# A hybrid decoder step on one core: the Pool mixer's map as a plain float32 product, with a new order of the pieces up to attention

## The chip, the cores and the metric

The kernel runs on one core of a Trainium2 chip. The metric is device microseconds of one execution, as the median of several runs. Times of single instructions come from one profiled execution of the same program, whose own time is given beside them.

## The reference

One layer with a prompt of 1024 tokens and eight sample tokens of one step each, which share the weights. Cut to what matters:

```python
h = rmsnorm(x, g_mix)
u = h @ w_in                              # 1024 -> 512 (a) + 512 (val) + 512 (gate)
a_ext = concat([pool_hist, a])            # group A: trailing windows of 2, 4, 8, 16 tokens
d = [win_sum_g / cnt_g - a_g for g in range(4)]        # 128 channels each
ya = (einsum('blgc,gcd->blgd', d, w_map) + b_map) * scale
yb = silu(layernorm(causal_conv31(val * sigmoid(gate))))    # group B
x = x + concat([ya, yb]) @ w_out
k, v = rmsnorm(mem) @ w_k, rmsnorm(mem) @ w_v          # 256 memory tokens, 4 heads
x = x + softmax(rmsnorm(x) @ w_q @ k.T / 16) @ v @ w_o
x = x + (silu(h2 @ w_gate) * (h2 @ w_up)) @ w_down     # h2 = rmsnorm(x)
y = rmsnorm(x, g_final)
```

The sample tokens go through the same products; their attention uses a cache of its own. All is float32. The outputs are y, the new states of the windows and of the convolution, and k and v.

## The kernel before

**Layout.** Channels lie on the 128 partitions, tokens along the free axis: T = 1032 columns, the 512 even and the 512 odd tokens of the prompt and the 8 samples. A product over all tokens is made in three pieces of 344 columns.

**Three passes.** Operands of products are split into a high and a low half in the reduced type fp32r, and a product is the sum of three passes (high x high, high x low, low x high). `step3` (L457) emits them: nine matmuls of 344 columns for one 128x128 block of a weight. The high half of a tensor is a copy on ACT or POOL (L346, L348), the low half a subtraction on DVE or POOL (L357, L359). For some weight blocks the low half is made by DMA instead (`split_by_dma`, L362 on): the negated high half is written first (a second copy on ACT, L368, or POOL, L370), then a DMA issued by POOL (L375) adds the weight from HBM to it. NOT_BY_DMA and BY_DMA name the blocks.

**The planner.** Each step is given to `Program.add` with the engines that can do it, a cost on each, what it reads and what it writes. `Program.order` then lists all steps by a simulated time: it takes the step that can start first, the earlier created one among near equals, and gives each an engine and a buffer. Every engine runs its instructions in the order so found, and the number of buffers of a kind (2 for product sums of the kind mm, 3 for raw weights, 2 for split weights, 19 large operands, 3 scratch) decides too when a step can start. So a cost moves no work by itself; it moves choices. ORDER is a string of pieces, in which they are created: A mixer inputs, g and v the gates and values of the convolution, C and D the convolution's taps (its sums `cacc` on DVE, L663), W windows, M the window's map, K and V keys and values of the memory, O and B the two halves of the output projection (`oa` and `ob`), L LayerNorm, q, S, T, P attention of the prompt, a to e that of the samples, Y and Z states. Behind ORDER stand the projection w_o, the gate stage and the down stage.

**Weights.** `w_take` hands over the next split block and keeps up to LEAD blocks more in preparation (`w_prep` splits, `w_load` fetches the raw block).

**The Pool mixer.** `windows` (L777) adds shifted copies of the input `a` for a window of 2, 4, 8 or 16 (L790 to L795, on POOL or DVE) and makes the mean minus the token itself (L802 to L804, always DVE): tile `win`. It is then split in two halves, tile `dop`. `mixer_out` (L841) multiplies `dop` by its block of the map (tile `pmap`, nine matmuls) and evicts with bias and scale on ACT (`yf`, L848); `yf` is split into `opa`, an operand of `oa` with the four blocks of w_out_a. The map's weight is one of the sequence of split blocks, between other weights.

**Beside it.** Keys (`kps`, L827) use a block of w_k for 24 matmuls of 256 columns; a piece K has two blocks. Values (`vps`, L901) use a block of w_v for 24 matmuls of 512 columns in two groups of 12; a piece V has four blocks. The LayerNorm of the convolution needs the sum of all its channels (`ysum`, L682), two products with a matrix of ones in plain float32 (`mean_ps`, L868, `rstd_ps`, L487) and gives the operands `opb` of `ob`.

Of the kernel before, what the change touches and what calls it, by code (L numbers as in the profile page):

```python
# [88 lines left out]
class Program:  # L89
# [4 lines left out]
    SIGNAL, SIGNAL_PE, SAME = 0.2, 0.29, {"DVE": 0.12, "ACT": 0.1}  # L94

    def __init__(self, capacity):
        self.capacity = capacity
        self.tasks, self.writer, self.readers, self.later = [], {}, {}, 0

    def add(self, engines, emit, r=(), w=(), lock=False, func=None, nbytes=0):  # L100
        t = Task()
        t.engines = engines
# [140 lines left out]
def hybrid_step_kernel(ctx: ExitStack, tc: tile.TileContext, io):  # L243
# [119 lines left out]
    def split_by_dma(dst, key, src, n, r, again, again_keys, pool_too=False):  # L363
# [11 lines left out]
        add({"Pool": 1.04}, lambda e: e.dma_start(dst(1), again(), accum_op=ALU.add), [key(1)] + again_keys, [key(1)], nbytes=4 * P * n)  # L375
# [31 lines left out]
    def w_load():  # L407
        i = state["loaded"]
        if i >= state["upto"]:
            return  # L410
        name, j = seq[i]
        width = 512 if name == "pool_map" else 1024
        raw = buf(f"raw{i}", "raw", (P, 1024))
        dma(lambda: raw[:, :width], lambda: io[name][j][:, :width], 512 * width, w=[(raw,)])
        raws[i] = (raw, width)
        state["loaded"] += 1

    def w_prep():
        i = state["prepped"]
        raw, width = raws.pop(i)  # L420
        name, j = seq[i]
        w = buf(f"w{i}", "op" if name in WIDE or i >= len(seq) - 4 else "w", (P, 2, 1024), F32R)
        if name in BY_DMA and i not in NOT_BY_DMA:
            split_by_dma(lambda p: w[:, p, :width], lambda p: (w, p), lambda: raw[:, :width], width, [(raw,)],
                         lambda: io[name][j][:, :width], [], name not in ("w_dn", "w_dn2"))
        else:
            split(lambda p: w[:, p, :width], lambda p: (w, p), lambda: raw[:, :width], width, [(raw,)])
        preps[i] = w
        state["prepped"] += 1
# [21 lines left out]
    def step3(ps, w, wkeys, cols, x, k, first, last, spans=range(NCH), keys=None):  # L451
# [8 lines left out]
        add({"PE": 0.146 * 3 * len(spans)}, emit, list(wkeys) + (keys or [(x, 0), (x, 1)]),  # L460
# [313 lines left out]
    a2 = [op_buf(f"a{i}") for i in range(2)]  # L774
    dops = {}

    def windows(g):  # L777
# [3 lines left out]
        tmp = op_buf(f"win{g}")  # L781
        add({"DVE": 0.07}, lambda e: e.tensor_copy(st_pool()[:, g, :, 15], ab[:, ai, SEQ:T]), [ak, (side, "pool")], [(side, "pool", g)])
# [24 lines left out]
        dops[g] = op_r(f"dop{g}")  # L807
        split(lambda p: dops[g][:, p], lambda p: (dops[g], p), cur, T, [ck])
# [11 lines left out]
    def keys(q):  # L820
        ps = mm_buf(f"kps{q}", 1)
        for i in range(2):
            w, wkeys = w_take("w_k")
            for k in range(KT):
# [4 lines left out]
                add({"PE": 0.327}, emit, wkeys + [(memg[k // 4], p, k % 4) for p in range(2)], [(ps,)])  # L829
# [62 lines left out]
    def values(c):  # L892
        ps = mm_buf(f"vps{c}", 2)
        for kk in range(4):
            w, wkeys = w_take("w_v")
            for k in (2 * kk, 2 * kk + 1):
# [6 lines left out]
                add({"PE": 1.3}, emit, wkeys + [(memg[k // 4], p, k % 4) for p in range(2)], [(ps,)])  # L903
# [76 lines left out]
    def scores(n):  # L980
# [23 lines left out]
        add({"PE": 1.31}, emit, [(qop[2 * h + dt], p) for dt in range(2) for p in range(2)] + [(kk, p, o) for p in range(2)], [pk])  # L1004
# [42 lines left out]
    def pv(n):  # L1047
# [4 lines left out]
        for c in range(2):  # L1052
# [8 lines left out]
            add({"PE": 1.3}, emit, [(v, 0), (v, 1)] + [(pT[h][m], p, c) for p in range(2) for m in range(2)], [(ps, c)])  # L1061
# [209 lines left out]
    def product(w, cols, xs, steps=1):  # L1271
# [254 lines left out]
    rsqrt_rows("Rf", Rf, RF, xss2, [(xss2,)], ones_d, 0, T)  # L1526
    for f in range(AHEAD):
        first_two(f)
    for f in range(FF_TILES):
# [5 lines left out]
        else:  # L1535
            fixed["DVE"] = 0.148
# [28 lines left out]

    last_w = {block: w_take(block[0]) for block in last_blocks}
# [3 lines left out]
    def last_down(c, n):  # L1570
# [19 lines left out]
        for w, keys, ks in ((wa, ka, range(4)), (wb, kb, (4, 5))):  # L1590
            add({"PE": 0.000425 * 3 * len(ks) * width}, lambda e, ks=ks: emit(e, ks),
# [148 lines left out]
```

## Time and profile before

| | us |
|---|---|
| median of 3 runs | 1251.86 (1251.17 to 1253.36) |
| the profiled execution | 1254.77 |
| its span, first to last instruction | 1252.9 |
| TensorE busy | 1215.9 |
| VectorE (DVE) busy | 926.7 |
| ScalarE (ACT) busy | 529.7 |
| GpSimd (POOL) busy | 458.8 |

The span is what the profiler records between the first and the last instruction; the execution's time also has what lies around it. In the rows of the profile PE is TensorE's matmuls, PEld its weight loads, SP the engine that issues most DMAs. A name such as `pmap<-dop,w` gives the tile written and the tiles read, L457 the line of the kernel. What stands in brackets behind a row is the time for which the engine was idle ahead of it, and what ended that.

### The profile page before, as it was taken

What the parts mean: (1) busy time and instruction counts of PE and PEld (TensorE: products, weight loads), DVE (VectorE), ACT (ScalarE), POOL (GpSimd) and SP (SyncE); (2) the same over time, 40 slices, a digit from 0 to 9 for tenths busy, and PEclk for the clock granted to TensorE, in tenths of its full rate; (3) what the DMA queues carried; (4) which work ended last, traced back from release to release, by engine and by line L of the source; (5) the groups of instructions that cost most, each with busy time, mean ns of one, the idle gap of its engine ahead of it and who ended that gap; (6) DMA issues with size and microseconds to landing.
All of it is one profiled execution on the core that took longest, in us unless ns stands there. A gap on an engine that the chain in (4) does not pass through costs nothing.

```text
span 1252.9 us, 22090 instructions
## 1 busy us (share of the span) xinstructions
PE 1215.9 (97%) x8958; PEld 1194.3 (95%) x8958; DVE 926.7 (74%) x1564; ACT 529.7 (42%) x731; POOL 458.8 (37%) x407
## 2 busy tenths in 40 slices
PE   8999996999999999999999999999999999999996
PEld 8999976999999879999999999999999999999996
DVE  7899988657367777679778677866867887778644
ACT  7766648454223453344322222222222364433644
POOL 3577841021101002113422233133324477778401
PEclk9999997999999999999999999999999999999998
DMA  7447686734255664231331332223322597778703
GB/s 281 104 84 169 142 241 177 213 88 163 104 194 207 238 225 169 102 132 38 112 126 60 111 110 102 104 67 111 106 85 89 205 312 198 206 181 206 175 26 111
DMA packets 59157, 183.86 MB, mean 147 GB/s; under 512 B 7920, under 2 KB 11696, under 8 KB 57776
## 3 DMA queue, kind: packets, MB, share of 16 engines
q1 hardware_dynamic: 52288, 157.74, 36.4%
q0 software_dynamic: 6768, 24.72, 11.2%
q8 instruction: 70, 1.15, 0.4%
q14 instruction: 31, 0.25, 0.1%
HBM read 148.80 MB, written 33.64 MB: 146 GB/s over the span
## 4 chain that ended last, share of the span: by engine, by line
PE 73%; DVE 10%; issue 7%; DMA 5%; ACT 2%; POOL 2%; SPq 0%; DVEq 0%; POOLq 0%; ACTq 0%
PE pr L1290 45%; PE ps L457 11%; PE fd L1587 6%; PE oa L457 4%; PE ob L457 4%; DVE cacc L663 2%; DMA raw<-in_w_v 2%; PE sc L1000 1%; DVE spcache_v L1097 1%; DMA spcache_k<-in_cache_k 1%; POOL w L357 1%; PE pv L1058 1%; DVE spcache_k L1097 1%; DMA w<-in_w_in 1%; DVE xss L384 1%
## 5 line engine op out<-in xcount | busy, mean ns | idle before, releaser
L1305 DVE TENSOR_TENSOR su<-pr,su 128x258 f32<-128x258 f32 (+1 forms) x204 | 109.3, 558 | 71.0 <-PE pr L1290 69.9
L1290 PE MATMUL pr<-ab,wTa 128*128 128x258 f32 x1056 | 134.2, 283 | 0.8 <-DVE su L1305 0.8
L1290 PE MATMUL pr<-ab,wG 128*128 128x258 f32 x1056 | 133.9, 283 | 0.8 <-ACT wU L346 0.8
L1290 PEld LDWEIGHTS pr<-ab,wTa 128*128 128x128 f32 x1056 | 130.1, 189 | 1.0 <-issue 1.0
L1290 PEld LDWEIGHTS pr<-ab,wG 128*128 128x128 f32 x1056 | 129.8, 189 | 1.2 <-ACT wU L346 1.1
L1290 PE MATMUL pr<-ab,wTb 128*128 128x258 f32 x1056 | 130.6, 283 | 0.0
L1290 PEld LDWEIGHTS pr<-ab,wTb 128*128 128x128 f32 x1056 | 128.6, 190 | 0.0
L457 PE MATMUL ps<-xop,w 128*128 128x344 f32 x720 | 114.1, 320 | 0.3 <-DMA w<-in_w_in 0.3
L457 PEld LDWEIGHTS ps<-xop,w 128*128 128x128 f32 x720 | 113.3, 188 | 0.6 <-DMA w<-in_w_in 0.6
L1290 PE MATMUL pr<-hb,dV 128*128 128x258 f32 x768 | 98.5, 284 | 1.1 <-ACT pp L1309 0.7
L1290 PEld LDWEIGHTS pr<-hb,dV 128*128 128x128 f32 x768 | 95.0, 189 | 1.8 <-ACT pp L1309 0.9
L457 PE MATMUL ps<-xq,w 128*128 128x344 f32 x576 | 94.8, 321 | 0.0
L457 PE MATMUL po<-oo,w 128*128 128x344 f32 x576 | 91.0, 320 | 0.4 <-DVE oo L1063 0.4
L457 PEld LDWEIGHTS po<-oo,w 128*128 128x128 f32 x576 | 90.7, 188 | 0.7 <-DVE oo L1063 0.7
L457 PEld LDWEIGHTS ps<-xq,w 128*128 128x128 f32 x576 | 90.6, 188 | 0.1
L1305 DVE TENSOR_TENSOR x<-pr,x 128x516 f32<-128x516 f32 (+1 forms) x122 | 63.3, 556 | 23.2 <-PE pr L1290 22.0
L663 DVE SCALAR_TENSOR_TENSOR cacc<-glu,vec,cacc 128x511 f32<-128x511 f32 (+14 forms) x116 | 77.0, 742 | 0.0
L1290 PE MATMUL pr<-hb,dW 128*128 128x258 f32 x576 | 75.0, 283 | 0.2 <-DVE x L1305 0.2
L1290 PEld LDWEIGHTS pr<-hb,dW 128*128 128x128 f32 x576 | 71.7, 189 | 0.4 <-DVE x L1305 0.4
L1587 PE MATMUL fd<-ho,w 128*128 128x258 f32 x576 | 70.0, 283 | 0.0
L346 ACT ACTIVATE w<-raw 128x1024 fp32r<-128x1024 f32 (+2 forms) x34 | 31.6, 932 | 90.2 <-issue 38.2
L1587 PEld LDWEIGHTS fd<-ho,w 128*128 128x128 f32 x576 | 69.5, 189 | 0.1
(323 smaller groups left out, 2338.5 us busy)
## 6 DMA issues: line engine op xcount, KB each, us to landing
gr<-in_w_gu SPq DMA_DIRECT2D x44, 512.0 KB, 3.4
hs<-hb SPq DMA_DIRECT2D x28, 516.0 KB, 4.2
hb<-su SPq DMA_DIRECT2D x8, 1032.0 KB, 4.9
dr<-in_w_dn SPq DMA_DIRECT2D x16, 512.0 KB, 6.2
hb<-hb POOLq DMA_DIRECT2D x12, 516.0 KB, 7.8
spcache_k<-in_cache_k SPq DMA_DIRECT2D x12, 512.0 KB, 5.0
raw<-in_w_in SPq DMA_DIRECT2D x10, 512.0 KB, 5.3
w<-in_w_in POOLq DMA_DIRECT2D x9, 512.0 KB, 6.6
```

Of the source, the lines that this page charges most:

```text
L346: e.activation(dst(0), src(), AF.Copy, scale=1.0 if gain is None else gain)
L357: e.tensor_tensor(dst(1), src(), f32(dst(0)), ALU.subtract)
L384: add({"Pool": pool_tt(n), "DVE": dve(n)}, lambda e: e.tensor_tensor(total(), total(), sq[:, i, :n], ALU.add), [(sq, i), tkey], [tkey], lo ...
L457: e.matmul(ps[:, c, :CW], w[:, wi, cols], x[:, xi, c * CW : (c + 1) * CW], start=first and p == 0, stop=last and p == 2)
L663: e.scalar_tensor_tensor(acc[h][:, n:], src[:, : HALF - n], w, acc[h][:, n:], ALU.mult, ALU.add)
L1000: e.matmul(bank()[:, i * NMEM : (i + 1) * NMEM], qop[2 * h + dt][:, qi, tt * P : (tt + 1) * P], kk[:, ki, 2 * (h % 2) + dt], start=(dt == ...
L1058: e.matmul(ps[:, c], v[:, vi, m, col : col + P], pT[h][m][:, pi, sl], start=(m == 0 and p == 0), stop=(m == 1 and p == 2))
L1097: e.scalar_tensor_tensor(piece[:, b], piece[:, b], 1.0, bc[:, b], ALU.mult, ALU.mult, accum_out=out(m)[:, first + b : first + b + 1])
L1290: e.matmul(bank(c), w[:, wi, cols(j)], xs[0](j, xi)[:, c * TQ : (c + 1) * TQ], start=j == 0 and p == 0, stop=j == nj - 1 and p == 2)
L1305: from_sums(sums, "DVE", dve, lambda e, src, sl: e.tensor_tensor(as_banks(o(sl), src), src, as_banks(a(sl), src), ALU.add), [akey], [okey])
L1587: e.matmul(view(i), w[:, wi, col : col + P], hops[k][:, xi, lo + i * width // count : lo + (i + 1) * width // count], start=(k == 0 and p ...
```

## The change

**The map.** `windows` no longer splits its result. `mixer_out` multiplies the float32 tile `win` by the map's float32 weight in plain float32, three matmuls of 344 columns for a group in place of nine of reduced type. The weight is loaded once, unsplit, into a large operand buffer when the first window is made, and leaves the sequence of split blocks.

**ORDER** is written anew up to attention and within it. Among others K2 now stands ahead of V1 and V0, and the maps M stand later against the values.

**Low halves by DMA** are named block by block: w_k 1, 2, 3, 5, 7 (before 0 to 5 and 7), w_v 0, 1, 3, 5, 7 (before 0, 1, 5), w_out_a 0, 1, 3 (before all four), w_out_b 2 and 3 (before 0 and 1), w_q 0, 3, 6 and w_o 4, 5, 6 (before none). For w_in and the down weights the same blocks remain.

**Leads and costs.** LEAD is 3 for w_k (4 before), 1 for w_out_a (3), 9 for w_q (5), 8 for w_out_b and w_o (5). Raw loads are given a lower priority (BIAS). The planner's costs of TensorE are written as functions with a factor of 0.93 in the first and the last stage, a signal of TensorE costs 0.35 (0.29), a subtraction on POOL 0.05 more, POOL's issue of a DMA 0.6 (1.04).

```diff
-    "A3 n0 g1 v1 C0 m0 g2 v2 m3 C1 m7 s0 m4 m6 g3 v3 m5 A2 A0 m1 s1 A1 m2 s2 K0 W3 K1 V1 V0 s3 W1 C2 W0 W2 K2 "
...
+    "m4 m7 A3 n0 g1 m0 v1 g2 v2 g3 m2 m3 m6 C0 m5 C1 m1 v3 A2 A0 s1 A1 s0 K0 s2 K1 W3 K2 V1 W0 W1 D0 s3 V0 M1 M0 "
...
-NOT_BY_DMA = (0, 1, 2, 16, 18, 19, 22, 23, 26, 27, 35, 36, 53, 54)
-BY_DMA = ("w_in", "w_k", "w_v", "pool_map", "w_out_a", "w_out_b", "w_dn", "w_dn2")
+BY_DMA = {"w_in": (0, 1, 2, 3, 4, 5, 6, 7, 9, 10, 11), "w_k": (1, 2, 3, 5, 7), "w_v": (0, 1, 3, 5, 7), "w_out_a": (0, 1, 3), "w_out_b": (2, 3), "w_q": (0, 3, 6), "w_o": (4, 5, 6), "w_dn": (17, 18, 19), "w_dn2": (1,)}
-LEAD = {"w_k": 4, "w_v": 3, "pool_map": 1, "w_out_a": 3, "w_q": 5, "w_in": 2, "w_out_b": 5, "w_o": 5}
+LEAD = {"w_k": 3, "w_v": 3, "w_out_a": 1, "w_q": 9, "w_in": 2, "w_out_b": 8, "w_o": 8}
-BIAS = {"evac": 10, "prep": 20, "load": 0}
+BIAS = {"evac": 10, "prep": 20, "load": 60}
+MARGINS = {
+    "early": {"PE": (0.93, 0.0)},
+    "gated": {},
+    "down": {"DVE": (1.0, 0.083)},
+    "last": {"PE": (0.93, 0.0), "DVE": (1.0, 0.083)},
+}
...
-    SIGNAL, SIGNAL_PE, SAME = 0.2, 0.29, {"DVE": 0.12, "ACT": 0.1}
+    SIGNAL, SIGNAL_PE, SAME = 0.2, 0.35, {"DVE": 0.12, "ACT": 0.1}
...
+    def pe(n, count=1):
+        return (0.006 + 0.00044 * n) * count
+
+    def pe32(n):
+        return 0.01 + 0.0017 * n
...
     def pool_tt(n):
-        return 0.09 + 0.00216 * n
+        return 0.14 + 0.00216 * n
...
-        add({"Pool": 1.04}, lambda e: e.dma_start(dst(1), again(), accum_op=ALU.add), [key(1)] + again_keys, [key(1)], nbytes=4 * P * n)
+        add({"Pool": 0.6}, lambda e: e.dma_start(dst(1), again(), accum_op=ALU.add), [key(1)] + again_keys, [key(1)], nbytes=4 * P * n)
...
-        if name in BY_DMA and i not in NOT_BY_DMA:
+        if j in BY_DMA.get(name, ()):
...
+    wmap = op_buf("wmap", (P, 512))
     dops = {}
...
+        if not dops:
+            dma(lambda: wmap[:], lambda: io["pool_map"][0], 512 * 512, w=[(wmap,)])
...
-        dops[g] = op_r(f"dop{g}")
-        split(lambda p: dops[g][:, p], lambda p: (dops[g], p), cur, T, [ck])
+        dops[g] = cur, ck
...
-        if not opa:
-            state["wm"] = w_take("pool_map")
-        wmap, wmk = state["wm"]
         ps = mm_buf(f"pmap{g}")
-        step3(ps, wmap, wmk, block_cols(g), dops[g], 0, True, True)
+        cur, ck = dops[g]
+
+        def emit(e):
+            for c in range(NCH):
+                e.matmul(ps[:, c, :CW], wmap[:, block_cols(g)], cur()[:, c * CW : (c + 1) * CW], start=True, stop=True)
+
+        add({"PE": NCH * pe32(CW)}, emit, [(wmap,), ck], all3(ps))
```

Where the maps stand on TensorE, before: from the last block of V0 (`vps`) over the keys K2 and K3 (`kps`) to the first group of `oa`. Numbers behind a name tell buffers apart.

```order
L901 MATMUL vps_1803<-w_1747,memg_370 128x512 x12
L827 MATMUL kps_1888<-memg_335,w_1760 128x256 x12
L827 MATMUL kps_1888<-memg_370,w_1760 128x256 x12
L827 MATMUL kps_1888<-memg_335,w_1821 128x256 x12
L827 MATMUL kps_1888<-memg_370,w_1821 128x256 x12
L457 MATMUL pmap_1958<-dop_1734,w_1801 128x344 x9
L457 MATMUL pmap_1982<-dop_1861,w_1801 128x344 x9
L457 MATMUL pmap_1997<-dop_1935,w_1801 128x344 x9
L827 MATMUL kps_2023<-memg_335,w_1947 128x256 x12
L827 MATMUL kps_2023<-memg_370,w_1947 128x256 x12
L457 MATMUL pmap_2052<-dop_2018,w_1801 128x344 x9
L827 MATMUL kps_2023<-memg_335,w_1968 128x256 x12
```

And now, the same engine and place, from V0's first two blocks (`vps_1860`) to the last map; K2 stands ahead of these rows.

```order
L917 MATMUL vps_1860<-w_1736,memg_370 128x512 x12
L917 MATMUL vps_1860<-w_1820,memg_370 128x512 x12
L860 MATMUL pmap_1915<-win_1855,wmap 128x344 x3
L917 MATMUL vps_1860<-w_1885,memg_335 128x512 x12
L917 MATMUL vps_1860<-w_1895,memg_335 128x512 x12
L860 MATMUL pmap_1971<-win_1801,wmap 128x344 x3
L860 MATMUL pmap_1987<-win_1548,wmap 128x344 x3
L840 MATMUL kps_1996<-memg_370,w_1913 128x256 x12
L840 MATMUL kps_1996<-memg_335,w_1913 128x256 x12
L840 MATMUL kps_1996<-memg_370,w_1935 128x256 x12
L840 MATMUL kps_1996<-memg_335,w_1935 128x256 x12
L860 MATMUL pmap_2065<-win_1975,wmap 128x344 x3
```

Three maps stood in a row behind K2, and the fourth within K3; now one stands within V0, two behind it, and the fourth behind K3.

On VectorE, before, around the third window and the split of the second and third (`dop`; `vv` is the low half of the values):

```order
L357 TENSOR_TENSOR dop_1861<-win_1795,dop_1861 128x1032
L793 COPY win_1884<-a_1439 128x1
L794 TENSOR_TENSOR win_1884<-a_1439 128x511
L795 TENSOR_TENSOR win_1884<-a_1439 128x512
L802 TENSOR_TENSOR win_1884<-win_1884,cnt 128x2x8
L803 TENSOR_REDUCE win_1884<-side 128x8
L804 SCALAR_TENSOR_TENSOR win_1884<-win_1884,a_1439 128x1032
L357 TENSOR_TENSOR vv_1909<-vf_1892,vv_1909 128x1024
L793 COPY win_1943<-a_523 128x1
L794 TENSOR_TENSOR win_1943<-a_523 128x511
L795 TENSOR_TENSOR win_1943<-a_523 128x512
L357 TENSOR_TENSOR dop_1935<-win_1884,dop_1935 128x1032
```

And now, around the window of the first map (`win_1855`), behind the last taps `cacc`:

```order
L674 SCALAR_TENSOR_TENSOR cacc_0_1650<-glu_986,vec,cacc_0_1650 128x498
L674 SCALAR_TENSOR_TENSOR cacc_1_1658<-glu_986,vec,cacc_1_1658 128x498
L674 SCALAR_TENSOR_TENSOR cacc_0_1650<-glu_986,vec,cacc_0_1650 128x497
L816 TENSOR_TENSOR win_1855<-win_1855,cnt 128x2x8
L817 TENSOR_REDUCE win_1855<-side 128x8
L818 SCALAR_TENSOR_TENSOR win_1855<-win_1855,a_1438 128x1032
L371 TENSOR_TENSOR w_1885<-raw_1726,w_1885 128x1024
```

The subtractions for `dop` are gone, and the means stand behind all taps of the convolution's last channels, with a weight's low half next.

More of the change, by code (lines that the diff above doesn't have):

```diff
@@ L93 @@
     DMA_LATENCY, DMA_RATE, DMA_ISSUE, TABLE = 0.95, 0.36e6, 0.45, 1.28
-    SIGNAL, SIGNAL_PE, SAME = 0.2, 0.29, {"DVE": 0.12, "ACT": 0.1}
+    SIGNAL, SIGNAL_PE, SAME = 0.2, 0.35, {"DVE": 0.12, "ACT": 0.1}
     def __init__(self, capacity):
         self.capacity = capacity
-        self.tasks, self.writer, self.readers, self.later = [], {}, {}, 0
+        self.tasks, self.writer, self.readers, self.later, self.margin = [], {}, {}, 0, MARGINS["early"]
     def add(self, engines, emit, r=(), w=(), lock=False, func=None, nbytes=0):
         t = Task()
-        t.engines = engines
+        t.engines = {}
+        for e, cost in engines.items():
+            factor, more = self.margin.get(e, (1, 0)) if not nbytes else (1, 0)
+            t.engines[e] = cost * factor + more
         t.emit, t.lock, t.func, t.nbytes = emit, lock, func, nbytes
@@ L280, in ch3 @@
         return ap.rearrange("p (c n) -> p c n", c=NCH)
+    def pe(n, count=1):
+        return (0.006 + 0.00044 * n) * count
+    def pe32(n):
+        return 0.01 + 0.0017 * n
     def act(n, ps=False, ptrs=0):
         return (0.05 if ps else 0.093) + 0.000833 * n + 0.093 * ptrs
-    fixed = {"DVE": 0.065}
     def dve(n):
-        return fixed["DVE"] + 0.00105 * n
+        return 0.065 + 0.00105 * n
     def pool_tt(n):
-        return 0.09 + 0.00216 * n
+        return 0.14 + 0.00216 * n
     def pool_ts(n):
@@ L828, in emit @@
                                  start=(k == 0 and p == 0), stop=(k == KT - 1 and p == 2))
-                add({"PE": 0.327}, emit, wkeys + [(memg[k // 4], p, k % 4) for p in range(2)], [(ps,)])
+                add({"PE": pe(NMEM, 3)}, emit, wkeys + [(memg[k // 4], p, k % 4) for p in range(2)], [(ps,)])
         kf = scr(f"kf{q}", (P, 2, NMEM))
@@ L902, in emit @@
                                      start=(k == 0 and p == 0), stop=(k == KT - 1 and p == 2))
-                add({"PE": 1.3}, emit, wkeys + [(memg[k // 4], p, k % 4) for p in range(2)], [(ps,)])
+                add({"PE": pe(512, 6)}, emit, wkeys + [(memg[k // 4], p, k % 4) for p in range(2)], [(ps,)])
         vf = scr(f"vf{c}", (P, 2, 512))
@@ L1003, in scores @@
         o = 2 * (h % 2)
-        add({"PE": 1.31}, emit, [(qop[2 * h + dt], p) for dt in range(2) for p in range(2)] + [(kk, p, o) for p in range(2)], [pk])
+        add({"PE": pe(NMEM, 12)}, emit, [(qop[2 * h + dt], p) for dt in range(2) for p in range(2)] + [(kk, p, o) for p in range(2)], [pk])
         st = buf(f"sm{h}_{i2}", "sm", (P, 8))
@@ L1059, in emit @@
                                  start=(m == 0 and p == 0), stop=(m == 1 and p == 2))
-            add({"PE": 1.3}, emit, [(v, 0), (v, 1)] + [(pT[h][m], p, c) for p in range(2) for m in range(2)], [(ps, c)])
+            add({"PE": pe(512, 6)}, emit, [(v, 0), (v, 1)] + [(pT[h][m], p, c) for p in range(2) for m in range(2)], [(ps, c)])
             add({"ACT": act(512, True)}, lambda e, c=c, sl=sl: e.activation(oo[:, 0, sl], ps[:, c], AF.Copy), [(ps, c)], [(oo, 0, c)])
@@ L1526, in hybrid_step_kernel @@
     rsqrt_rows("Rf", Rf, RF, xss2, [(xss2,)], ones_d, 0, T)
+    pg.margin = MARGINS["gated"]
     for f in range(AHEAD):
@@ L1535, in hybrid_step_kernel @@
         else:
-            fixed["DVE"] = 0.148
+            pg.margin = MARGINS["down"]
             later(lambda: dn_load(0), "load")
@@ L1563, in hybrid_step_kernel @@
         hidden_load(f)
+    pg.margin = MARGINS["last"]
     last_w = {block: w_take(block[0]) for block in last_blocks}
```

21 lines of the change are left out of this document (9 added, 12 removed), and 6 rows, old and new, of the table ORDER.

## The prediction, made before the changed kernel ran

> **What bounds the kernel now.** I read the page first: how busy is the engine of the products, and where is it not?
>
> ```profile
> span 1252.9 us, 22090 instructions
> ...
> PE 1215.9 (97%) x8958; PEld 1194.3 (95%) x8958; DVE 926.7 (74%) x1564; ACT 529.7 (42%) x731; POOL 458.8 (37%) x407
> ...
> PEclk9999997999999999999999999999999999999998
> ```
>
> TensorE works 1215.9 of 1252.9 us, so only 37.0 us are idle. Of the 40 slices (31.3 us each) one in the middle was granted a clock of 7 tenths: the seventh, 188 to 219 us. Everything else is product after product, and a change that leaves the number of products nearly alone can gain little but idle time and lost clock. So the next view is TensorE's waits, largest first (waiting tile, line, what came last, total, times, longest).
>
> ```profile
> PE pmap L457 <- ACT yf L848: 4.9, 1, 4.9
> PE psg L457 <- ACT w L346: 4.9, 1, 4.9
> PE oa L457 <- ACT yf L848: 3.0, 1, 3.0
> PE pmap L457 <- ACT vf L906: 2.4, 1, 2.4
> PE kps L827 <- DMA w<-in_w_k: 1.9, 1, 1.9
> ```
>
> The second is the start of the program, which the change leaves. The first, third, fourth and fifth (4.9 + 3.0 + 2.4 + 1.9) belong to the map (pmap), the products behind it (oa) and the key product beside it (kps). TensorE's timeline there (start, length, what, records; in brackets the idle time ahead):
>
> ```profile
> 148.99 11.62 PE L827 MATMUL kps<-memg,w 128*128 128x256 f32 x96
> 160.44 22.27 PE L901 MATMUL vps<-w,memg 128*128 128x512 f32 x96
> 182.55 3.57 PE L827 MATMUL kps<-memg,w 128*128 128x256 f32 x26
> 187.98 2.86 PE L827 MATMUL kps<-memg,w 128*128 128x256 f32 x22 [1.86 <-DMA w<-in_w_k]
> 193.22 1.83 PE L457 MATMUL pmap<-dop,w 128*128 128x344 f32 x9 [2.37 <-ACT vf L906]
> 199.95 5.31 PE L457 MATMUL pmap<-dop,w 128*128 128x344 f32 x18 [4.91 <-ACT yf L848]
> 205.10 2.99 PE L827 MATMUL kps<-memg,w 128*128 128x256 f32 x24
> ...
> 208.79 1.21 PE L457 MATMUL pmap<-dop,w 128*128 128x344 f32 x6 [0.22 <-DVE dop L357]
> ...
> 215.84 15.80 PE L457 MATMUL oa<-opa,w 128*128 128x344 f32 x81 [3.02 <-ACT yf L848]
> 231.48 1.88 PE L868 MATMUL mean_ps<-ysum,ones_c 128*128 128x512 f32 x4
> 232.79 3.41 PE L457 MATMUL oa<-opa,w 128*128 128x344 f32 x18
> ...
> 244.79 2.19 PE L487 MATMUL rstd_ps<-vss,ones_c 128*128 128x512 f32 x6
> ```
>
> Until 182 us the stream has no gap. Then come five: 1.86 + 2.37 + 4.91 + 0.22 + 3.02 = 12.4 us, a third of all the idle time, in 33 us. And the products between them are slow. What such a record takes undisturbed, the chain that ended last tells for the next stage:
>
> ```profile
> 268.38 45.20 PE ob L457 x288
> ```
>
> 45.20 / 288 is 0.157 us. The 18 pmap records from 199.95 to 205.10 take 5.15 us where 18 x 0.157 is 2.8; the 81 oa records from 215.84 to 231.48 take 15.64 where 81 x 0.157 is 12.7. The windows say why (length, then busy time of PE, PEld, DVE, ACT, POOL, then granted clock, DMA share, GB/s):
>
> ```profile
> 175.00:200.00 25.00, 15.77 (x92) 13.39 (x90) 24.11 (x33) 17.15 (x21) 9.39 (x10) 0.89 0.80 212
> 202.00:204.00 2.00, 2.00 (x9) 2.00 (x8) 1.97 (x5) 1.06 (x1) 0.39 (x1) 0.50 0.58 69
> 216.00:218.00 2.00, 2.00 (x8) 2.00 (x9) 1.89 (x4) 2.00 (x4) 0.00 (x0) 0.50 1.00 204
> 222.00:224.00 2.00, 2.00 (x14) 2.00 (x14) 1.08 (x2) 0.00 (x0) 1.06 (x1) 1.00 1.07 422
> ```
>
> The granted clock is 0.50 at 202 to 204 and again at 216 to 218; at 222 it is whole. So the gaps cost twice: 12.4 us idle, and 2.3 + 2.9 us of half-speed products (5.15 - 2.8, 15.64 - 12.7), with some 0.3 us for the nine records at 193.22 (1.83 against 9 x 0.157 = 1.4). The stretch loses 12.4 + 5.5 = 17.9 us. The second spell stands behind a gap of 3.02 us, the first behind 1.86 and 2.37 with 5 us of products around them.
>
> The Trainium skill, "TensorE: Matmul & The Clock Gate" (HAM oscillation), says that only idle gaps above about 3.4 us throttle the array. The trace differs: 3.02 us was enough. By the page's rule new gaps under 3.4 us would cost only themselves; by the rows a gap of 3 us can cost 5.9 (3.02 and 2.9), the price of a spell below.
>
> What makes the gaps? In the first window VectorE works 24.11 of 25 us, and the map's path needs both it and ScalarE in their fixed order: window mean (DVE), high half (ACT), low half (DVE), three-pass product, eviction yf (ACT), then again two halves. The groups of the halves (busy in sum, mean ns, idle time ahead):
>
> ```profile
> L357 DVE TENSOR_TENSOR dop<-win,dop 128x1032 fp32r<-128x1032 f32 x4 | 4.9, 1230 | 2.8 <-ACT dop L346 2.8
> ...
> L346 ACT ACTIVATE dop<-win 128x1032 fp32r<-128x1032 f32 x4 | 4.2, 1055 | 6.8 <-DVE win L804 6.8
> ```
>
> and VectorE's timeline at the last window:
>
> ```profile
> 207.50 1.23 DVE L357 TENSOR_TENSOR dop<-win,dop 128x1032 fp32r<-128x1032 f32 x1 [2.75 <-ACT dop L346]
> ```
>
> VectorE waited 2.75 us for the high half, and TensorE's product then waited at 208.79 for this low half. So the present bound here is the chain of ACT and DVE around four short products, with TensorE waiting for it and then running at half clock.
>
> **The change part by part.** *The map.* It removes four high halves (4.2 us of ACT), four low halves (4.9 us of DVE) and the split of the map's weight; the product reads the window mean directly. 36 records of three passes become 12 plain float32 products over 344 columns. The trace has no such product of 344; the nearest rows are mean_ps, two products over 512 columns in four records. They take 1.88 us, or 1.31 up to the next group's start (231.48 to 232.79). That is 0.66 to 0.94 us for 512 columns, so 0.44 to 0.63 for 344 and 1.3 to 1.9 for a map of three, against 9 x 0.157 = 1.42 now. Four maps: from -0.4 to +1.9 us. I take +1.2, nearer the whole length of the row than its start to start, since records can be missing from the latter.
>
> The Trainium skill, "FP8 and Floating Point Precision" (TensorE Precision Notes), says that true float32 takes four passes through the array, against three here: 12 x 0.157 = 1.9 us for a map, an estimate from that page that lies at the upper end of the rows and would make the sum +1.9. It is the rule that speaks against this change; it prices it at 0.7 us more than I do.
>
> *The new order of the pieces.* K2 goes ahead of V1 and V0, and one map stands in the middle of V0, two behind it, one behind K3. So while windows and evictions run, TensorE has values to work on. With the groups' own lengths (the key pieces 11.45 us for two from 148.99, the value pieces 22.1 us for two from 160.44), TensorE works from 148.99 to 166.2 on three key pieces, to 177.3 on V1, to 182.8 on half of V0, then on the first map. Between 148.99 and 215.84 it now works 66.85 - 12.4 - 2.6 = 51.9 us at full clock; with +1.2 for the maps oa would start at 148.99 + 53.1 = 202.1 if nothing waited, and run at full clock. Before, it starts at 215.84 and then loses 2.9: a gain of 16.7 us (17.9 - 1.2). That is the most this stretch can give.
>
> What is late next? First, the mean of the window for the first map, win_1855. VectorE's rows ahead of it, from the eviction of the last mixer input on:
>
> ```profile
> 149.20 1.23 DVE L813 TENSOR_TENSOR a<-ps,Rx 128x1032 f32<-128x1032 f32 x1
> 172.89 7.86 DVE L663 SCALAR_TENSOR_TENSOR cacc<-glu,vec,cacc 128x504 f32<-128x504 f32 x12
> ```
>
> In the new order there stand 29 steps of cacc (29 x 7.86 / 12 = 19.0), two first ones, three window means (about 1.5 each: one operation over 1032 columns, 1.23 as dop's, and two small ones), and some 8 us of operations of 1.2 or 0.7: 33 us, so ready at 182 at the earliest, with the short idle waits of such a stretch 184 to 186, against 182.8 wanted: 0 to 3 us of wait. Second, the low parts.
>
> *Other blocks by DMA.* w_v goes from three to five of eight blocks, w_k from seven to five, w_out_a from four to three; w_q and w_o get three each. A low part by DMA costs one more ACT copy (about 1.06 us, as dop's high half of nearly the same size) and the queue's time, and saves one subtraction on DVE or Pool. The page's DMA issues:
>
> ```profile
> w<-in_w_v POOLq DMA_DIRECT2D x3, 512.0 KB, 7.5
> ```
>
> 7.5 us from issue to landing is as long as two and a half V blocks (11.05 / 4 = 2.76 us each). By the order on ACT and POOL the low part of w_1820 is issued behind two ACT copies and earlier DMAs, so it lands near 181 to 183 where 180.1 is wanted: 1 to 3 us of wait; the neighbours w_1589 and w_1895 0 to 1 each. Such waits overlap in part with the wait for win_1855, since a later start gives the rest its time. I take 3 us for all of it (from 0 to 8, plus one spell of half clock, 2.9, if a gap comes near 3 us).
>
> *LayerNorm and ob.* The mixer outputs' next stage, ob, must not wait when oa ends early:
>
> ```profile
> 228.55 1.23 DVE L682 TENSOR_TENSOR ysum<-ysum,y 128x1032 f32<-128x1032 f32 x1
> ```
>
> From ysum's end (229.7) to ob is 38.7 us, of which 23.6 lie behind rstd_ps at 244.79. In the new order the rows of DVE from the eviction at 149.2 to the last ysum come to some 57 us by their durations: 206 without idle, 209 to 212 with some. rstd_ps is then due near 226 to 229, and ob's operands 23.6 later, 250 to 252. oa, 288 records of 0.157 with the LayerNorm's products (268.38 - 215.84 less 2.9 = 49.6 us), starting at 205 ends at 254.7. So it hides, with 3 to 5 us to spare; without stalls in front (start at 202) it is about even.
>
> *The planner's numbers* (margins, signal cost, costs of POOL) move only choices of engine and order. From the gate stage on TensorE's row of products is the same but for places exchanged; DVE and POOL swap some subtractions in the down stage. I cost this at nothing: VectorE is 74% busy over the program and no product of the gate and down stages stands among the waits above, which are the five largest. From -1 to +2.
>
> *Attention.* w_q and w_o are prepared further ahead, three blocks of each by DMA. What TensorE loses there now is in the windows:
>
> ```profile
> 425.00:450.00 25.00, 21.20 (x138) 18.41 (x137) 18.61 (x52) 14.96 (x36) 3.62 (x10) 1.00 0.62 226
> 450.00:475.00 25.00, 23.98 (x127) 20.40 (x126) 21.85 (x88) 8.35 (x17) 0.57 (x2) 1.00 0.71 258
> ```
>
> 3.8 + 1.0 = 4.8 us idle, without loss of clock. The new order can win at most that or add as much: 0 taken, -4 to +4.
>
> The sum: 17.9 - 1.2 - 3 = 13.7, rounded to 13.5 us. The profiled execution takes 1254.77 us (span 1252.9 and 1.9 around it), 2.9 above the median of 1251.86; it would become 1241.3, and on the scale of the median 1238.4.
>
> **The rivals.** *A: new waits eat most.* The low parts of V0 and K3 come late by the full 8 us and one spell of half clock comes back: 16.7 - 8 - 2.9 = 5.8 gained, 1246. For it: the 7.5 us landing, DMA share 0.58 to 1.07 in these windows, and the wait of 1.86 that a DMA causes now. Against: two key blocks fewer use this path, and the maps no longer load ACT and DVE. *B: ob waits for LayerNorm.* If DVE's 57 us stretch as its work did before (it needs 80.6 elapsed from 149.2 to 229.7 now, with more in it), ysum comes at 220 instead of 210 and ob waits some 8: 5 to 6 gained, 1246. Against: some of the present idle time on DVE is the map's own, such as the 2.75 us ahead of 207.50. *C, the other side: attention's weights.* Six w_q and w_o blocks now need POOL's queue while sample caches use the DMA (share 0.62 to 0.71). If each comes late, TensorE, which takes blocks in order, pays each time: 6 x 4 = 24 us, less 13.5: 1262. It decides from 13.5 / 6 = 2.3 us late per block. For it: landing times of 7.5 and more; against: their lead rises to nine and eight blocks, as far as buffers allow. *D: the change doesn't remove the wait.* pmap waited for yf and vf, both ACT evictions, not for dop; if ACT's order still brings evictions late, the same gaps remain and the map's float32 costs 1.2: no change, about 1252. Against: the new order has V0 and K3 between maps. *E: how short a gap may be.* The forecast's 3 us of new waits are split over several gaps and cost only themselves. If they come as one gap near 3.02 us, a spell of 2.9 follows: 1241.3.
>
> By the Trainium skill's page on the clock gate, named above, E cannot be, since the gap stays under 3.4 us; the row of 3.02 us speaks for it.
>
> **How the numbers follow.** The forecast, with or without one spell (gain 10 to 17, attention -2 to +2): 0.63. A 0.15, B 0.06, both faster; C 0.11, slower; D 0.05, same. E is part of the forecast, with 0.25 of its 0.63. Measurements of this kernel tell about 0.2% (2.5 us) from no change. So faster 0.84, same 0.05, slower 0.11. The low end is 16.7 + 4 = 20.7 gained, 1231; the high end takes in A and B, down to 3 gained, 1249; D and C stay outside, with the rest of A 0.2 in all.
>
> **What would show it.** Right: TensorE's waits without pmap and oa for yf; the windows from 194 to 224 at a clock of 1.00; oa starting at 202 to 207 and ob at 250 to 256; maps of 1.3 to 1.9 us. Wrong: a wait of vps or kps on a DMA above 3 us with a clock of 0.5 behind it (A), ob waiting for opb (B), ps or po waiting for w_q or w_o (C), yf still named ahead of pmap and oa (D).

## The result and the profile after

The changed kernel takes 1254.80 us (median of 22 runs, 1250.89 to 1260.93), the kernel before 1252.19 in the same comparison (22 runs, 1250.26 to 1253.88). The ratio is 1.0022, with a 95% interval from 1.0013 to 1.0032: slower by about 2.8 us, where 13.5 us faster was forecast. Two things are to be seen beside the median. The spread grew from 3.6 to 10.0 us. And the profiled execution is one of the quicker ones (1252.1 us, span 1250.3), as that of before was slower than all of its 22 runs here (1254.77): read side by side, the two profiles show the change 5 us better than the medians.

Where the time went is read from the times at which TensorE starts each stage, in the two profiles and in two of the experiments below:

| TensorE starts | before | changed | e1 | e6 |
|---|---|---|---|---|
| oa (first half of w_out) | 215.84 | 209.73 | 209.90 | 205.31 |
| ob (second half) | 268.22 | 259.48 | 259.65 | 254.94 |
| gate stage | 558.04 | 548.20 | 548.49 | 543.80 |
| down stage | 1006.27 | 998.30 | 997.39 | 992.50 |
| its last blocks (fd) | 1170.89 | 1168.20 | 1162.65 | 1157.37 |
| end of TensorE | 1243.55 | 1240.89 | 1235.36 | 1230.03 |

The changed kernel is 9.8 us ahead at the gate stage, 8.0 at the down stage and 2.7 behind it: what the stretch before ob won is given back late, 1.9 us in the gate stage (450.1 against 448.2) and 5.3 in the down stage (169.9 against 164.6). The lead at ob, 8.7 us, is no accident of one execution: e1, e7, e8 and e9, whose early part is that of the changed kernel, start ob at 259.4 to 259.7 in their profiles, and e2, whose early part is that of before, at 268.29.

TensorE's waits in the changed kernel, largest first (waiting tile, line, what came last, total, times, longest):

```profile
PE pmap L860 <- DVE win L818: 5.0, 1, 5.0
PE psg L468 <- ACT w L360: 4.9, 1, 4.9
PE pr L1306 <- DVE x L1321: 3.0, 3, 1.8
PE oa L468 <- DVE kf L844: 1.4, 1, 1.4
PE pr L1306 <- ACT wG L360: 1.1, 1, 1.1
PE Rx_ps L498 <- DVE Rx_m L503: 1.1, 1, 1.1
PE pr L1306 <- DVE wG L371: 1.0, 1, 1.0
```

The evictions yf are gone from the list; one wait for a window's mean has come, and three rows of `pr`, the products of gate and down stage, at 1.0 and more, where before each such row came to 0.8 or less. TensorE's timeline in the stretch of the maps (start, length, what, records; idle time ahead):

```profile
149.10 17.32 PE L840 MATMUL kps<-memg,w 128*128 128x256 f32 x144
166.26 16.82 PE L917 MATMUL vps<-w,memg 128*128 128x512 f32 x72
188.06 3.56 PE L860 MATMUL pmap<-win,wmap 128*128 128x344 f32 x6 [4.99 <-DVE win L818]
190.91 6.32 PE L917 MATMUL vps<-w,memg 128*128 128x512 f32 x24
197.07 3.63 PE L860 MATMUL pmap<-win,wmap 128*128 128x344 f32 x12
200.78 5.82 PE L840 MATMUL kps<-memg,w 128*128 128x256 f32 x48
206.43 1.90 PE L860 MATMUL pmap<-win,wmap 128*128 128x344 f32 x6
209.73 8.80 PE L468 MATMUL oa<-opa,w 128*128 128x344 f32 x54 [1.40 <-DVE kf L844]
```

Two gaps are left of five, 6.4 us of 12.4. A plain float32 map takes 3.71 / 2 = 1.85 us (197.07 to 200.78 for two). The first one takes 2.85 and the values behind it 6.16, where 24 such records take some 5.5 at full clock (22.1 / 96 x 24 before): behind the gap the granted clock is 0.57 (length, busy time of PE, PEld, DVE, ACT, POOL, then clock, DMA share, GB/s):

```profile
188.00:190.00 2.00, 1.94 (x4) 1.28 (x5) 1.97 (x3) 0.00 (x0) 1.84 (x1) 0.57 0.09 16
190.00:192.00 2.00, 2.00 (x5) 1.23 (x5) 1.93 (x4) 0.34 (x1) 0.00 (x0) 0.57 0.52 186
```

Why the mean came so late is in VectorE's and POOL's timelines of the changed kernel:

```profile
173.31 4.25 DVE L818 SCALAR_TENSOR_TENSOR win<-win,a 128x1032 f32<-128x1032 f32 x1
...
177.77 2.79 DVE L818 SCALAR_TENSOR_TENSOR win<-win,a 128x1032 f32<-128x1032 f32 x1
...
186.57 1.23 DVE L818 SCALAR_TENSOR_TENSOR win<-win,a 128x1032 f32<-128x1032 f32 x1
```

```profile
173.56 1.66 POOL L808 TENSOR_TENSOR win<-a 128x511 f32<-128x511 f32 x1
174.80 1.66 POOL L809 TENSOR_TENSOR win<-a 128x512 f32<-128x512 f32 x1
...
177.57 1.89 POOL L805 TENSOR_TENSOR win<-win 128x1022 f32<-128x1022 f32 x1
```

The same mean takes 1.23 us alone, and 4.25 and 2.79 while POOL adds for the next window: 4.6 us more in VectorE's row, nearly the wait of 5.0, since the mean of the first map's window (186.57) stands behind both. The taps `cacc`, which ran beside POOL's additions just before, kept their 0.65 us.

In the down stage the longest wait is this, on VectorE and on TensorE:

```profile
1034.61 5.15 DVE L371 TENSOR_TENSOR hb<-hs,hb 128x1032 fp32r<-128x1032 f32 x3
1039.68 0.68 DVE L1321 TENSOR_TENSOR x<-pr,x 128x516 f32<-128x516 f32 x1
```

```profile
1034.10 4.49 PE L1306 MATMUL pr<-hb,dV 128*128 128x258 f32 x36
1040.41 4.59 PE L1306 MATMUL pr<-hb,dW 128*128 128x258 f32 x24 [1.83 <-DVE x L1321]
```

Three low halves of hb (the operand of the down products) stand in a row on VectorE, each 1.7 us, and behind them the eviction x of a finished product, whose buffer TensorE needs for the next sums (there are two of this kind): it waits 1.83 us. Then its 24 records take 4.39 us (1040.41 to 1044.80) where the 36 records ahead of them at full clock took 4.49; the granted clock has fallen to a half:

```profile
1042.00:1044.00 2.00, 2.00 (x11) 2.00 (x11) 0.70 (x1) 1.49 (x3) 2.00 (x2) 0.50 0.94 347
```

The order is not all of this wait. The same operation takes 1.23 us in e1 (below, at 1032.39), and in the changed kernel POOL adds and subtracts beside the three (the tile `dt`, four operations from 1034.47 to 1040.33): 1.5 us of their 5.15 look like the effect seen at the means, and no run separates the two. In the whole down stage TensorE is idle 4.8 us where it was 1.4 before, and busy 165.1 where it was 163.3 with the same products.

### The profile page after: what moved, and what is told of

The parts are those of the page before. It is cut to its first block, busy times and chain, and to the rows that moved or that the text cites. A ratio compares the mean times of both kernels' runs of the same rounds, so it can differ in the third digit from the quotient of the medians.

```text
span 1250.3 us, 22052 instructions
## 1 busy us (share of the span) xinstructions
PE 1215.8 (97%) x8946; PEld 1191.1 (95%) x8946; DVE 926.4 (74%) x1551; ACT 519.8 (42%) x724; POOL 479.1 (38%) x422
## 4 chain that ended last, share of the span: by engine, by line
PE 51%; DVE 3%; issue 1%; DMA 0%; ACT 0%; DVEq 0%; SPq 0%; ACTq 0%
PE pr L1306 45%; PE fd L1605 6%; DVE hb L371 1%; DVE x L1321 0%; DMA hs<-hb 0%; DVE dW L371 0%; DVE su L1347 0%; DVE dV L371 0%; DVE pp L1329 0%; DVE x L1629 0%; ACT hb L360 0%; DVE pp L1321 0%; PE fin_ps L498 0%; DVE su L1321 0%; DVE ab L373 0%
## 5 line engine op out<-in xcount | busy, mean ns | idle before, releaser
L1306 PE MATMUL pr<-ab,wU 128*128 128x258 f32 x528 | 67.4, 284 | 0.0
```

The lines of the kernel that those rows point to most:

```text
L1306: e.matmul(bank(c), w[:, wi, cols(j)], xs[0](j, xi)[:, c * TQ : (c + 1) * TQ], start=j == 0 and p == 0, stop=j == nj - 1 and p == 2)
```

## The experiments

All ratios are to the kernel before, timed beside each experiment on the same chip. The changed kernel's own ratio is 1.0022.

**Which part of the program holds the loss.** Two kernels cross the early part of one with the planner's numbers of the other from the gate stage on; two more take the map alone.

e1: the changed kernel, late numbers as before. `stage` is set where the gate stage's steps begin.

```diff
-BIAS = {"evac": 10, "prep": 20, "load": 60}
+BIAS = {"evac": 10, "prep": 20, "load": 60, "load_late": 0}
...
-    "last": {"PE": (0.93, 0.0), "DVE": (1.0, 0.083)},
+    "last": {"DVE": (1.0, 0.083)},
...
-        return 0.14 + 0.00216 * n
+        return (0.09 if pg.stage else 0.14) + 0.00216 * n
...
-        add({"Pool": 0.6}, lambda e: e.dma_start(dst(1), ...
+        add({"Pool": 1.04 if pg.stage else 0.6}, lambda e: e.dma_start(dst(1), ...
...
-                signal, same = self.SIGNAL_PE if e == "PE" else self.SIGNAL, ...
+                signal, same = (0.29 if t.stage else 0.35) if e == "PE" else self.SIGNAL, ...
```

> The changed kernel, but the planner works from the gate stage on with the numbers of the kernel before (POOL's subtraction and DMA issue, TensorE's signal, raw loads' priority, margins); up to there all is as changed. Theory: the change wins some 9 us up to ob (259.48 against 268.38 in the two profiles) and loses them again in the gate's preparation and the down stage, because the new numbers put other work ahead of the evictions there. Then this kernel takes 1243 to 1246 us, and the waits of pr on x in the down stage are near those of before (0.7, 0.4, 0.2 us). Rival: the down stage loses because all arrives some 9 us earlier and meets other transfers, whatever the numbers: then 1253 to 1256.

Measured: 1246.81 us, ratio 0.9955 (0.9942 to 0.9968). That is 0.8 us above the theory's range and far from the rival's, which falls. Its waits for x in the down stage, and VectorE's row at the same place:

```profile
PE pr L1308 <- DVE x L1323: 1.1, 3, 0.5
```

```profile
1032.39 1.23 DVE L373 TENSOR_TENSOR hb<-hs,hb 128x1032 fp32r<-128x1032 f32 x1
1033.54 1.96 DVE L1323 TENSOR_TENSOR x<-pr,x 128x516 f32<-128x516 f32 x4
1035.41 1.79 DVE L373 TENSOR_TENSOR hb<-hs,hb 128x1032 fp32r<-128x1032 f32 x1
```

Evictions stand between the halves, and the down stage takes 165.3 us. In the two profiles e1 ends 5.5 us ahead of the changed kernel, in the medians 8.4: the rest is not in these two traces, since the changed kernel's profile is one of its quicker executions.

e2: the kernel before, with the changed numbers from the gate stage on (the same edit the other way round).

> The kernel before, with the changed planner numbers from the gate stage on only; up to there nothing is changed. Theory: slower by what the changed kernel loses behind ob, 7 us in its profile and more on average: 1258 to 1264, with waits of pr on x as in the changed kernel, and a wider spread of the runs. Rival (arrival time): as before, 1251 to 1254.

Measured: 1269.27 us, ratio 1.0123 (1.0110 to 1.0136), more than the theory's range. The waits for x are those of the changed kernel; beyond them TensorE waits for the last weights:

```profile
PE fd L1594 <- ACT w L351: 6.3, 1, 6.3
...
PE pr L1295 <- DVE x L1310: 2.9, 3, 1.8
```

In the changed kernel the wait ahead of fd is 0.8. So the numbers cost 8 us there (1.0022 against 0.9955) and 15 here (1.0123), by where each order happens to be tight. Both signs speak for the theory, the size does not carry over. The wider spread that was expected too did not come: the four runs lie within 2.6 us. Why the last weights are late by 6.3 us stays open.

e3: the changed kernel, map in three passes.

```diff
-    wmap = op_buf("wmap", (P, 512))
+    wraw, wmap = buf("wmap_raw", "raw", (P, 1024)), op_r("wmap", (P, 2, 512))
...
-            dma(lambda: wmap[:], lambda: io["pool_map"][0], 512 * 512, w=[(wmap,)])
+            dma(lambda: wraw[:, :512], lambda: io["pool_map"][0], 512 * 512, w=[(wraw,)])
+            split(lambda p: wmap[:, p], lambda p: (wmap, p), lambda: wraw[:, :512], 512, [(wraw,)])
...
-        dops[g] = cur, ck
+        dops[g] = op_r(f"dop{g}")
+        split(lambda p: dops[g][:, p], lambda p: (dops[g], p), cur, T, [ck])
...
+        step3(ps, wmap, [(wmap, 0), (wmap, 1)], block_cols(g), dops[g], 0, True, True)
```

> The changed kernel with the map in three passes again (window mean split in two halves, the map's weight split once in a large buffer); order of the pieces, blocks by DMA and numbers as changed, and the program from attention on the same instruction by instruction. Theory: plain float32 costs 1.85 us a map against 1.42, so 1.7 us in all, but spares the two halves (1.05 and 1.23 us) that would lie between the first window's mean and its map, which TensorE already waits for by 5.0 us: net slower by 0 to 4 us than the changed kernel, 1255 to 1259. Rival: the halves hide behind V0 and the four passes are what is seen: faster by 1.7, 1253.

Measured: 1270.04 us, ratio 1.0131 (1.0114 to 1.0148): far slower than either theory said. It waits in other places:

```profile
PE vps L913 <- DMA w<-in_w_v: 8.8, 2, 4.9
...
PE pmap L468 <- DVE dop L371: 4.1, 1, 4.1
```

The largest of these waits is not from the halves of the windows: TensorE waits 4.9 us for a low half of w_v until 174.57, and the first high half of a window is made on ACT at 179.35. This edit also splits the map's weight, which takes one of the three buffers of raw weights; POOL makes its halves from 149.26 to 152.04, and the first low half of w_v is issued at 165.96, where the changed kernel issues it at 159.14. That this buffer is the cause is likely and not shown. The wait for dop of 4.1 us is from the halves. ob starts at 272.9, 4.7 us behind the kernel before.

e4: the kernel before, with only the map plain; its edit is that of the change in `windows` and `mixer_out`, and the map's weight leaves the sequence of split blocks.

> The kernel before with the map as a plain float32 product, and nothing else changed (old order of the pieces, old blocks by DMA, old numbers); from attention on the same instructions. Theory: the first and the fourth map no longer wait for halves, ACT is free of four copies that stood ahead of the evictions yf, so the gaps of 4.9 and 3.0 us shrink: 1246 to 1250. Rival: the gaps come from the evictions and from TensorE having nothing else to do between three maps in a row, so they stay and float32 costs 1.7: 1253 to 1255.

Measured: 1249.88 us, ratio 0.9974 (0.9963 to 0.9984), as the theory had it; of the waits for yf, 3.1 and 1.3 us are left. ob starts at 262.8, 5.4 us earlier than before. So of the 8.7 us up to ob the map alone gives 5.4 with the old order, blocks and numbers. All the rest of the change, with a map in three passes as e3 makes it, loses 4.7, and with the plain map the two together give 8.7. The gains are not a sum of two: in these runs the rest of the change wins only with a map that needs no halves and no raw buffer.

**What is left in the stretch of the maps.** e5: the changed kernel with two pieces exchanged, so that the map within V0 takes a window that is ready.

```diff
-... s3 V0 M1 M0 W2 C2 C3 D1 D2 M3 K3 ...
+... s3 V0 M3 M0 W2 C2 C3 D1 D2 M1 K3 ...
```

> The changed kernel with two pieces of the order exchanged, M3 and M1: the map within V0 now takes the window whose mean is ready at 177.6 us in the changed kernel's profile, and the window that TensorE waited for until 188.06 comes behind V0. Everything from attention on is the same instruction by instruction. Theory: the 5.0 us of wait for win and the spell of lower clock behind it (some 1.6 us) go: 1247.5 to 1250. Rival: VectorE is the bound of the whole stretch, or the low halves of V0 come late, so that the wait only moves to the next value block or map: 1253 to 1256.

Measured: 1251.95 us, ratio 0.9987 (0.9976 to 0.9999), 4.4 us better than the changed kernel, but above the theory's range. The wait for win is gone, but others came, as the rival had it in part:

```profile
PE kps L840 <- DMA w<-in_w_k: 2.8, 1, 2.8
...
PE vps L917 <- DVE w L371: 1.1, 1, 1.1
```

e10: the changed kernel with the low halves by DMA for the blocks of before.

```diff
-... "w_k": (1, 2, 3, 5, 7), "w_v": (0, 1, 3, 5, 7), "w_out_a": (0, 1, 3), "w_out_b": (2, 3), "w_q": (0, 3, 6), "w_o": (4, 5, 6) ...
+... "w_k": (0, 1, 2, 3, 4, 5, 7), "w_v": (0, 1, 5), "w_out_a": (0, 1, 2, 3), "w_out_b": (0, 1) ...
```

> The changed kernel with the low halves by DMA for the same blocks as before (w_k 0 to 5 and 7, w_v 0, 1, 5, w_out_a all, w_out_b 0 and 1, none of w_q and w_o); order of the pieces, map and numbers as changed; from the gate stage on the same instructions. Theory: two more low halves of w_v on VectorE or POOL, 1.2 to 2.7 us each, in the stretch in which the window's mean is waited for, so the wait for win grows by 1 to 4 us: ratio 1.003 to 1.006, 1256 to 1260. Rival: the choice of blocks does nothing there: 1.000 to 1.003.

Measured: 1260.86 us, ratio 1.0059 (1.0042 to 1.0077). The size is the theory's, its reason is not: the wait for win is gone, and TensorE waits for low halves by DMA.

```profile
PE oa L468 <- DMA w<-in_w_out_a: 6.1, 1, 6.1
...
PE vps L917 <- DMA w<-in_w_v: 4.1, 2, 3.4
```

ob starts 4.8 us later than in the changed kernel (264.27). So the new choice of blocks is worth some 4.6 us with the new order, by not having these waits.

e11: the changed kernel with the additions of two windows on VectorE alone.

```diff
-            add({"Pool": pool_tt(SEQ) + 0.1, "DVE": dve(SEQ) + 0.08}, emit, [ck], [nk], lock=True)
+            add({"DVE": dve(SEQ) + 0.08} if g < 2 else {"Pool": pool_tt(SEQ) + 0.1, "DVE": dve(SEQ) + 0.08}, emit, [ck], [nk], lock=True)
```

> The changed kernel with the shifted additions of the two windows of group 0 and 1 on VectorE alone instead of on POOL. Theory: VectorE's window means took 4.25 and 2.79 us instead of 1.23 because POOL was adding for the next window at the same time; without that they take 1.2 to 1.3, and although VectorE has some 4 us more to do, the mean is ready near 183 and the wait of 5.0 us for win goes: ratio 0.997 to 0.999, 1248 to 1251. The means also move ahead of the last nine taps of the convolution in VectorE's row, which helps in the same direction. Rival: VectorE's means are slow for another reason, so they still take 3 to 4 us and the wait stays or grows: 1.002 to 1.006.

Measured: 1255.39 us, ratio 1.0018 (1.0006 to 1.0029), no gain, where the theory had 0.997 to 0.999. The last step of each mean is quick, and TensorE's wait has moved:

```profile
172.97 1.23 DVE L818 SCALAR_TENSOR_TENSOR win<-win,a 128x1032 f32<-128x1032 f32 x1
...
176.94 1.23 DVE L818 SCALAR_TENSOR_TENSOR win<-win,a 128x1032 f32<-128x1032 f32 x1
...
183.03 1.23 DVE L818 SCALAR_TENSOR_TENSOR win<-win,a 128x1032 f32<-128x1032 f32 x1
```

```profile
165.66 14.04 PE L917 MATMUL vps<-w,memg 128*128 128x512 f32 x60
184.36 3.48 PE L860 MATMUL pmap<-win,wmap 128*128 128x344 f32 x6 [4.67 <-issue]
```

The mean is ready 3.5 us earlier, near 184.2 instead of 187.7; but the planner, seeing that, put the map one value block earlier (60 records of values ahead of it, not 72), and TensorE waits 4.67 us again. There is the same effect again, too: the first step of the third mean, 0.16 us in the changed kernel, takes 2.34 here, beside a subtraction that POOL runs from 180.36 to 182.86.

```profile
180.56 2.34 DVE L816 TENSOR_TENSOR win<-win,cnt 128x16 f32<-128x16 f32 x1
```

That POOL's additions slow the means is shown by the durations, that the wait goes with them is not.

**Which numbers lose the time late.** e7 sets only POOL's subtraction back to 0.09 from the gate stage on, e8 only POOL's DMA issue to 1.04, e9 the subtraction and TensorE's signal (0.29). Each is one or two of the lines of e1's diff.

> The changed kernel with one number as before from the gate stage on: the cost of a subtraction on POOL (0.09 in place of 0.14 plus the columns); in the order, VectorE's row of three low halves of hb ahead of the evictions becomes two, and behind them rather than ahead. Theory: this number is what puts them on VectorE and makes most of the late loss: 1247 to 1250. Rival: the cheaper DMA issue of POOL does: 1253 to 1256.

> The changed kernel with one other number as before from the gate stage on: POOL's issue of a DMA costs 1.04 in place of 0.6. In the order, the three low halves of hb in a row become two, but behind three low halves of dW and dV. Theory: little is won, 1252 to 1255, since the row of VectorE's work ahead of the evictions is as long. Rival: the DMA issue is the cause: 1247 to 1250.

> The changed kernel with two numbers as before from the gate stage on: the cost of a subtraction on POOL (as in e7_late_subtraction_cost, 1250.8) and the signal of TensorE (0.29 in place of 0.35). Theory: the signal's number puts the first gate products ahead of their weight's halves (waits for wG of 1.3 and 1.0 us in e7, sometimes with a spell of lower clock behind them, none in e1); so this kernel is as e1_late_as_before, ratio to the kernel before 0.995 to 0.997, 1247 to 1249, with no wait for wG. Rival: those waits come from the other numbers: as e7, 0.9975 to 0.999.

Measured: e7 1250.76 us, ratio 0.9978 (0.9968 to 0.9989); e8 1256.50, 1.0030 (1.0017 to 1.0044); e9 1247.02, 0.9951 (0.9938 to 0.9965). By the ratios the subtraction's cost is 0.44% (5.5 us of the 8), the signal another 0.27% (3.4 us), and with both (e9) all is won that e1 wins with all the numbers. The DMA issue alone wins nothing: e8 is within the noise of the changed kernel. e7 and e8 lie 0.8 and 1.5 us above the ranges of their theories, e9 at the lower end of its own. In e8 TensorE waits for x as in the changed kernel and longer; in e7 the wait for x is down to 0.3 and that for the gate's weight stays; in e9 the first is 0.5 and the second gone:

```profile
PE pr L1308 <- DVE x L1323: 4.3, 3, 2.4
```

```profile
PE pr L1308 <- ACT wG L362: 1.3, 1, 1.3
...
PE pr L1308 <- DVE wG L373: 1.0, 1, 1.0
```

**A version that beats both.** e6 is e1 with e5's exchange.

> Both edits on the changed kernel: the old planner numbers from the gate stage on (as in e1_late_as_before, 1246.8) and M3 and M1 exchanged (as in e5). Theory: they act in different stages and add up: 5 to 6.5 below e1, 1240 to 1242. Rival: as for e5, 1246 to 1248.

Measured: 1241.25 us (1241.16 to 1244.29), ratio 0.9913 (0.9901 to 0.9926). The two edits add up: 0.42% below e1, as e5 is 0.35% below the changed kernel. Its largest waits behind the start of the program are two of 1.2 us, for weights of values and keys.

**Why the runs spread.** The changed kernel, e3, e5, e10 and e11 have the same instructions from the gate stage on. In each profile the same 24 products follow the gap at the three halves of hb. Here are e10 and e11, to be read beside the changed kernel's row at 1040.41:

```profile
1048.70 3.14 PE L1306 MATMUL pr<-hb,dW 128*128 128x258 f32 x24 [1.85 <-DVE x L1321]
```

```profile
1043.07 3.15 PE L1306 MATMUL pr<-hb,dW 128*128 128x258 f32 x24 [2.40 <-DVE x L1321]
```

3.14 us behind a gap of 1.85, 3.15 behind 2.40, but 4.59 behind 1.83 in the changed kernel's profile; in e3 and e5 it is slow too (behind 1.83 and 2.00). Three of five executions pay some 1.5 us more for a gap of about the same length. (e2, another program, has a gap of 1.80 at the same place and then 3.17.) The gate's two gaps (1.1 and 1.0) bring a lower clock in the windows of e5, e10 and e11 and none in those of the changed kernel and e3. Each gap is thus a draw, and the late part of the changed kernel holds several. The runs fit this: the five spread over 6.2 to 10.0 us (4 to 22 runs each), and e1, e6 and e9, which have neither gap, over 1.9 to 3.8 (5 or 6 runs). Against it stands e2, with gaps for x as long and a spread of 2.6 in four runs. That the 10 us are nothing but such draws is argued from this, and not shown run by run.

## Why the prediction was wrong

**The bound and the place.** Right. The gaps at the maps cost 12.4 us and the clock, and the change removes half of the gaps and the longer spells: oa starts 6.1 us earlier, and runs at full clock, so ob starts 8.7 earlier. The forecast had 13.7 here. Of the 17.9 us, the maps took 1.8, the two gaps that are left 6.4 (3 were taken for all new waits), and the slow spell behind the first 1.6, which leaves some 8.

**The map's price.** Mis-sized by a third, though inside the bounds given (1.3 to 1.9 us a map): 1.85 us against 1.41 before, 1.8 us in all where 1.2 was taken. The rule of the Trainium skill, "FP8 and Floating Point Precision" (TensorE Precision Notes), of four passes gave 1.9 and is what the trace shows.

**VectorE ahead of the first map.** The step "33 us, so ready at 182 at the earliest, [...] 184 to 186" failed: 187.7. It took each operation at its length alone. Two means beside POOL's additions added 4.6 us. A row of the kernel before showed that a length can stretch, and was not used: a copy of two columns on VectorE (L790, else 0.16 us) took 4.05 at 180.65, and ended at 184.70 with POOL's operation L646 (184.67). The Trainium skill, "GPSIMD Engine Reference" (Specifications), says that POOL shares its SBUF interfaces with VectorE, with contention for operations of two SBUF inputs: the means are such, and the taps, with one input in PSUM, were not slowed. The trace agrees for these; the copy above has a single input.

**Low halves by DMA.** The step with "1 to 3 us of wait" for w_1820 failed the other way: no value block waits for a DMA in the changed kernel, and the old choice of blocks would have cost 4.6 us more (e10). The waits of rival A, for low halves by DMA, did not come.

**LayerNorm and ob.** Right that it hides: ob starts without a gap, at 259.5, not 250 to 256, since oa itself started at 209.7 and not at 205. Rival B falls with it.

**Attention.** No change was taken; from ob to the gate stage the changed kernel takes 288.7 us against 289.8. Rival C falls.

**The planner's numbers.** This is the step that failed: "I cost this at nothing [...] From -1 to +2." By e1 they cost 0.67%, 8.4 us. The reason given, that VectorE is 74% busy and that no product of these stages stood among the waits, is true of the order before and says nothing about another one. With two buffers for such sums, a row of three operations ahead of an eviction is enough. The differences in VectorE's and POOL's order in the down stage were seen and taken as an exchange of equals. No rival had this mechanism. A priced 5.8 us of gain, nearly the 5.6 (0.45%) that e1 keeps, for another reason; D's 1252 is nearest to what was measured, and that is luck, since the waits for yf that it was to keep are gone. Nor would the forecast have held without this step: e1 gains 5.6 us by the medians (8.2 by the two profiles) against 13.5. The shortfall up to ob is 5 of the rest; the profile of before, from which the gain was read, lies 2.6 us above its median, in a stage that is not known.

**The clock.** The price "a gap of 3 us can cost 5.9" was a maximum, not a price: gaps of 1.8 to 2.4 brought a slow spell three times in five, some 1.5 us. The rule of 3.4 us of the Trainium skill's page, "TensorE: Matmul & The Clock Gate" (HAM oscillation), warns of longer gaps; it is no safe bound here, as the row at 1040.41 shows, with a clock of 0.50 behind a gap of 1.83. The same page says (Part 1) that the window in which activity is counted runs freely and doesn't start with the kernel; the five executions, with the same gap now slow and now not, fit that.

## What to carry to other kernels

Numbers of a planner are an edit to every stage that it plans: cost the order that they make in the stages which the change doesn't mean to touch, above all what now stands ahead of the evictions of a full product buffer. A gain at one place and a loss at another are told apart in one look by the times at which each stage starts, and proven by crossing the halves of the two kernels. And where VectorE and POOL run side by side, an operation's length when alone is only its lower bound.

## What the runs showed of the hardware

- An operation of VectorE with two operands in SBUF (1032 columns, 1.23 us) took 4.25 and 2.79 us while POOL ran additions of 511 to 1022 columns, ending some 1.1 us behind POOL's; 1.23 again with POOL's additions taken away (e11). In e11 one of 16 columns took 2.34 us in place of 0.16 beside a subtraction of POOL. Not every such pair is slow: in the changed kernel a subtraction of 1024 columns that VectorE starts at 187.72, just ahead of a copy on POOL (187.91 to 189.84), takes its 1.22 us.
- A gap of TensorE of 1.83 us was followed by 24 products in 4.59 us, gaps of 1.85 and 2.40 us before the same products by 3.14 and 3.15: the length of the gap alone does not decide.
- A plain float32 product of 344 columns takes 0.62 us (1.85 / 3) at full clock, four times the 0.157 of one reduced pass.
